# Gate and up blocks of an encoder layer: third and fourth products summed in a bank of their own

## The chip, the cores and the metric

The kernel runs on one core of a Trainium2 chip. The core has five engines that run their own instruction queues in order: PE (TensorE, matrix products), DVE (VectorE), ACT (ScalarE), POOL (GpSimd) and SP (SyncE, which here only issues DMAs). PE's weight loads have rows of their own, PEld. Products land in PSUM, in banks of 128 x 512 float32 values. The metric is the device time of one execution in microseconds (us).

## The reference, cut to what matters

One layer of a hybrid encoder works on two sequences of 512 tokens by 1024 channels. It starts and ends with a SwiGLU feed-forward step of 2816 hidden channels; between them lies a mixing stage (attention and a matrix memory) that the change does not touch.

```python
def swiglu(x, w_gate, w_up, w_down):
    return (jax.nn.silu(x @ w_gate) * (x @ w_up)) @ w_down
...
x = x + 0.5 * swiglu(rms_norm(x, ffn1_norm), ffn1_w_gate, ffn1_w_up, ffn1_w_down)
...
x = x + 0.5 * swiglu(rms_norm(x, ffn2_norm), ffn2_w_gate, ffn2_w_up, ffn2_w_down)
```

## The kernel before

Matrices are kept as a high and a low part in a reduced float32 type, and one product of values costs three matmuls (high by high, high by low, low by high). `product` (line 333) makes one block product: 4 slices of 128 channels by 3, so 12 matmuls of 128x512 into one bank.

Gate and up are computed together by a scheme of seven products in place of eight for a 2 x 2 block product: the two sequences are the two columns, the halves of the 1024 channels the inner index, and gate and up the two rows. The seven are called B11, B21, B22, T1, T2, T3 and T4. A block is 128 of the 2816 hidden channels; there are 22 blocks, and each feed-forward step runs them all before its down phase (line 589), which reads the products' sides back from HBM (`rbuf`).

For ten of the blocks, 0 to 9, B11 and B21 are computed early, while the inputs of the others are still being prepared, and parked in HBM (`kept`). Their turn later is called a *resumed* block here: its parked pieces v1 and g0 are loaded and it computes five products, T2, T1, T3, B22, T4. The other twelve, *computed* blocks, run all seven: B11, T2, B21, T1, T3, B22, T4. `ORDER` alternates the two kinds (0, 10, 1, 11 ... 7, 17), then come 18 to 21, computed, and 8 and 9, resumed.

`gu_rest` sums a block. It has three banks of PSUM pools: X (pool "mm", three buffers, `MM`) for B11 and B21, Y (pool "s", named pss, two buffers, `PS`) and Z (pool "t", named pst, two buffers, `PT`). One more pool, "o" (named pso, one buffer, `PO`), is used by the mixing stage and by the down phase. In a timeline X reads mm, Y pss and Z pst; T4's rows are those whose weights are called f.

The steps that the prediction names, all in `gu_rest`: line 364 (DVE) adds v1 and Y; line 368 (ACT) copies Z, with T1 in it, to v5; line 372 (DVE) adds the bank with T3 to v5; line 374 adds v1 to v5; line 377 (DVE) makes u2 from the bank Z, which by then holds T1 and B22; line 382 (DVE) adds the bank with T4 to v1; lines 383 and 384 multiply gate and up. Lines 291 and 292 split weights into high and low parts on ACT and DVE, lines 314 to 320 make their sums and differences, line 672 and 673 split T4's weights (and down weights), lines 396 and 397 split the block's results for the down phase and 398 and 399 store them through SP, and 403 to 415 form sums of the results of two blocks.

A scheduler orders each engine's queue from estimated times and priorities; the steps under `shifted(SOONER)` come ahead of others that are ready, those under `shifted(LATER)` behind. SP's queue carries the loads and stores.

Of the kernel before, what the change touches and what calls it, by code (L numbers as in the profile page):

```python
# [12 lines left out]
ALU = mybir.AluOpType  # L13
# [13 lines left out]
def encoder(ctx, tc, I, outs):  # L27
# [14 lines left out]
    def nm(s):  # L42
        n_id[0] += 1
        return f"{s}_{n_id[0]}"

    @contextmanager
    def shifted(n):

        tc.cur_priority += n
        yield  # L50
        tc.cur_priority -= n
# [58 lines left out]
    def PO():  # L110
        return po_.tile([P, S], F32, tag="o", name=nm("pso"))

    def PS():
        return ps.tile([P, S], F32, tag="s", name=nm("pss"))

    def PT():
        return pt.tile([P, S], F32, tag="t", name=nm("pst"))
# [149 lines left out]
    V_ = nc.vector  # L267
# [3 lines left out]
    B11, B21, B22, T4, T1, T2_, T3 = range(7)  # L271
# [29 lines left out]
    def w8_tile():  # L301
        return wpool.tile([P, 2, 2, HK_, P], F32R, tag="w8", bufs=4, name=nm("w"))

    def gu_left_a(rg, pin=lambda i: i):

        wa = w8_tile()
        w_pair(wa, rg.rearrange("p (a k) c -> p a k c", a=2), pin)
        return {B11: part(wa, 0), B21: part(wa, 1)}
# [20 lines left out]
    def product(p, w, xt, first):  # L329
        wh, wl = w  # L330
        for k in range(HK_):
            for i, (a, b) in enumerate(((wh, 0), (wh, 1), (wl, 0))):
                nc.tensor.matmul(p, a[:, k, :], xt[:, b, k, :], start=(first and k == 0 and i == 0),  # L333
                                 stop=(k == HK_ - 1 and i == 2), skip_group_check=True)

    def gu_first_a(W, xc, v1):

        X = MM()
        product(X, W[B11], xc[B11], True)
        with shifted(SOONER):  # L340
            nc.scalar.activation(v1, X, AF.Copy)
        return X

    def gu_first_b(X, W, xc, g0):

        product(X, W[B21], xc[B21], False)
        with shifted(SOONER):
            nc.scalar.activation(g0, X, AF.Silu)

    def gu_rest(W, xc, got, ring, mid):  # L350

        Y, Z = PS(), PT()
        second = lambda: product(Y, W[T2_], xc[T2_], True)
        if got:
            v1, g0 = got
            second()
        else:
            v1, g0 = ring("v"), ring("h")
            X = gu_first_a(W, xc, v1)
            second()  # L360
            gu_first_b(X, W, xc, g0)
        u2 = ring("h")
        with shifted(SOONER):
            V_.tensor_tensor(u2, v1, Y, op=ALU.add)  # L364
        product(Z, W[T1], xc[T1], True)
        v5 = ring("v")
        with shifted(SOONER):
            nc.scalar.activation(v5, Z, AF.Copy)  # L368
        mid()
        product(Y, W[T3], xc[T3], False)  # L370
        with shifted(SOONER):
            V_.tensor_tensor(v5, v5, Y, op=ALU.add)
        with shifted(SOONER):
            V_.tensor_tensor(v5, v5, v1, op=ALU.add)
        product(Z, W[B22], xc[B22], False)
        with shifted(SOONER):
            V_.tensor_tensor(u2, u2, Z, op=ALU.add)
        with shifted(SOONER):
            nc.scalar.activation(u2, u2, AF.Silu)
        product(Y, W[T4], xc[T4], False)  # L380
        with shifted(SOONER):
            V_.tensor_tensor(v1, v1, Y, op=ALU.add)
        V_.tensor_tensor(g0, g0, v1, op=ALU.mult)
        V_.tensor_tensor(u2, u2, v5, op=ALU.mult)
        return g0, u2
# [40 lines left out]
    class Up:  # L426
# [34 lines left out]
        def rest(self, raw, at=None, hook=None):  # L461
# [12 lines left out]
            for i, j in enumerate(ORDER):  # L474
                W = left
                nxt = ORDER[i + 1] if i + 1 < NF else None
                if nxt is not None:
                    left = {} if nxt in self.kept else gu_left_a(raw[0])
                    left.update(gu_left_b(*raw, ring))
                    ru = raw[1]  # L480
                    raw = self.fetch(ORDER[i + 2]) if i + 2 < NF else None
                then = []
                h = gu_rest(W, self.xc, got, ring, lambda: then.append(resume(nxt)) if nxt in self.kept else None)
                got = then[0] if then else None
                if nxt is not None:
                    left.update(gu_left_c(ru, ring))
                if i % 2 == 0:
                    sides = Sides(self.rb[i // 2], ring)
                    with shifted(LATER):
                        sides.even(*h)  # L490
                elif i < NF - 1:
                    sides.odd(*h)
                if i == at:
                    hook(h[0])
# [748 lines left out]
    xc = [None] * 7  # L1243
# [100 lines left out]
    W = [w8_tile() for _ in range(2)]  # L1344
# [15 lines left out]
    W = [{B11: part(w, 0), B21: part(w, 1)} for w in wt]  # L1360
# [11 lines left out]
    def second(j):  # L1372
        product(X[j], W[j][B21], xc[B21], False)
# [90 lines left out]
    xc = [None] * 7  # L1464
# [27 lines left out]
    W = [gu_left_a(raw0[0])]  # L1492
# [140 lines left out]
```

## Time and profile before

| | us |
|---|---|
| median of three runs | 2075.32 (2074.75 to 2075.62) |
| profiled execution | 2074.45 |
| its span | 2072.7 |
| PE busy | 2059.4 (99%) |
| DVE busy | 1544.9 (75%) |
| ACT busy | 903.3 (44%) |
| first gate and up stage, from the first T2 of a resumed block | 76.1 to 443 |
| second gate and up stage, likewise | 1481.6 to 1848 |

A row of a timeline has the start and the length in us, engine, line and operation, the tile written and the tiles read, shapes, and how many equal instructions it joins (x12); idle time of the engine ahead of a row stands in brackets, with what ended it. A matmul's length is drawn to its end, past the start of the next one, so lengths of neighbours overlap and starts tell the pace. In a view of waits a row names who waited (engine, tile, line), for whom, the total in us, how often, and the longest.

### The profile page before, as it was taken

How to read it: one execution, taken by the hardware profiler on the slowest of the kernel's cores; microseconds unless marked ns; L12 is line 12 of the kernel's file. 1: busy time of each engine (PE TensorE's matmuls, PEld its weight loads, DVE VectorE, ACT ScalarE, POOL GpSimd, SP SyncE). 2: the span in 40 equal slices, each digit the busy share in tenths (PEclk: the TensorE clock that was granted, in tenths of full speed). 3: DMA queues.
4: the chain of work that ended last, by engine and by line, in shares of the span. 5: the costliest groups of instructions: out<-in, count | busy, mean ns of one | idle time of the engine just before them, and what ended most of it. 6: DMA issues, size and time to landing. Idle time of an engine off the chain costs nothing.

```text
span 2072.7 us, 27121 instructions
## 1 busy us (share of the span) xinstructions
PE 2059.4 (99%) x9454; PEld 1689.0 (81%) x9454; DVE 1544.9 (75%) x2783; ACT 903.3 (44%) x1649; POOL 101.7 (5%) x117
## 2 busy tenths in 40 slices
PE   9999999999999999999999999999999999999998
PEld 7888888888888877888878788888888888888887
DVE  7888988786797897675567646555888888796697
ACT  7544444443234566463345443324544444443224
POOL 0000000001003000000120000002000000000001
PEclk9999999999999999999999999999999999999999
DMA  9555655699766655767684345677656555599753
GB/s 317 180 193 174 209 169 179 209 343 355 263 224 245 213 156 179 263 233 272 209 282 165 106 150 189 206 254 243 205 170 215 185 181 183 169 347 347 272 204 122
DMA packets 308104, 454.84 MB, mean 219 GB/s; under 512 B 20072, under 2 KB 179904, under 8 KB 306944
## 3 DMA queue, kind: packets, MB, share of 16 engines
q1 hardware_dynamic: 305968, 447.39, 64.0%
q0 software_dynamic: 1840, 5.46, 0.8%
q8 instruction: 74, 1.21, 0.2%
q14 instruction: 62, 0.51, 0.1%
q10 hardware_dynamic: 160, 0.27, 0.0%
HBM read 286.15 MB, written 166.89 MB: 219 GB/s over the span
## 4 chain that ended last, share of the span: by engine, by line
PE 97%; DVE 1%; DMA 1%; ACT 1%; issue 0%; ACTq 0%
PE mm L771 21%; PE pss L333 18%; PE pst L333 12%; PE mm L333 11%; PE mm L589 8%; PE pst L589 4%; PE pss L589 4%; PE mm L755 4%; PE pso L589 3%; PE pss L1018 1%; PE pso L1045 1%; PE pso L755 1%; PE pst L1037 1%; PE pso L1181 1%; PE pst L771 1%; PE pss L771 1%
## 5 line engine op out<-in xcount | busy, mean ns | idle before, releaser
L771 PE MATMUL mm<-xh,w 128*128 128x512 f32 x896 | 290.4, 394 | 0.0
L333 PE MATMUL mm<-xc,w 128*128 128x512 f32 x1056 | 254.5, 392 | 2.9 <-DVE w L292 1.6
L333 PE MATMUL pss<-xc,w 128*128 128x512 f32 x1056 | 256.0, 391 | 0.0
L333 PE MATMUL pst<-xc,w 128*128 128x512 f32 x1056 | 253.8, 389 | 0.0
L333 PEld LDWEIGHTS mm<-xc,w 128*128 128x128 f32 x1056 | 198.5, 189 | 45.6 <-DVE w L292 2.0
L333 PEld LDWEIGHTS pss<-xc,w 128*128 128x128 f32 x1056 | 197.0, 188 | 46.7 <-DVE t L364 6.1
L333 PEld LDWEIGHTS pst<-xc,w 128*128 128x128 f32 x1056 | 198.2, 188 | 41.5 <-ACT t L368 0.4
L771 PEld LDWEIGHTS mm<-xh,w 128*128 128x128 f32 x896 | 167.7, 188 | 33.5
L589 PE MATMUL mm<-rt,w 128*128 128x512 f32 x765 | 178.9, 389 | 0.0
L771 PE MATMUL mm<-xl,w 128*128 128x512 f32 x448 | 176.3, 394 | 0.0
L589 PEld LDWEIGHTS mm<-rt,w 128*128 128x128 f32 x765 | 143.5, 188 | 29.8
L291 ACT ACTIVATE w<-t 128x512 fp32r<-128x512 f32 x176 | 106.8, 627 | 136.4 <-issue 55.2
L292 DVE TENSOR_TENSOR w<-t,w 128x512 fp32r<-128x512 f32 x176 | 117.9, 687 | 55.3 <-ACT w L291 53.4
L333 PE MATMUL pss<-xc,f 128*128 128x512 f32 x528 | 126.8, 389 | 0.0
L333 PEld LDWEIGHTS pss<-xc,f 128*128 128x128 f32 x528 | 99.1, 188 | 20.6
L672 ACT ACTIVATE w<-wr 128x512 fp32r<-128x512 f32 x72 | 45.1, 632 | 138.5 <-PE pso L589 64.9
L672 ACT ACTIVATE w<-t 128x512 fp32r<-128x512 f32 x82 | 51.8, 632 | 107.3 <-PE pst L589 62.4
L771 PEld LDWEIGHTS mm<-xl,w 128*128 128x128 f32 x448 | 84.3, 188 | 16.7
L589 PE MATMUL pss<-rt,w 128*128 128x512 f32 x396 | 93.7, 389 | 0.0
L589 PE MATMUL pst<-rt,w 128*128 128x512 f32 x396 | 93.7, 389 | 0.0
L239 ACT ACTIVATE w<-wr 128x1024 fp32r<-128x1024 f32 (+1 forms) x56 | 57.3, 1028 | 73.5 <-PE mm L771 30.3
L589 PEld LDWEIGHTS pss<-rt,w 128*128 128x128 f32 x396 | 74.3, 188 | 15.4
(379 smaller groups left out, 3649.5 us busy)
## 6 DMA issues: line engine op xcount, KB each, us to landing
rt<-rbuf SPq DMA_DIRECT2D x154, 512.0 KB, 5.5
wpark<-w SPq DMA_DIRECT2D x104, 512.0 KB, 3.5
w<-wpark SPq DMA_DIRECT2D x104, 512.0 KB, 4.6
wr<-in_ffn_w_gate_dram SPq DMA_DIRECT2D x62, 512.0 KB, 5.3
rbuf<-tab SPq DMA_DIRECT2D x102, 256.0 KB, 3.8
wr<-in_ffn_w_up_dram SPq DMA_DIRECT2D x44, 512.0 KB, 4.4
rbuf<-f SPq DMA_DIRECT2D x72, 256.0 KB, 4.0
wr<-in_w_in_dram SPq DMA_DIRECT2D x36, 512.0 KB, 6.0
```

The lines of the kernel that those rows point to most:

```text
L239: pin(nc.scalar.activation(hi, raw, AF.Copy))
L291: pin(nc.scalar.activation(t[:, 0], src, AF.Copy))
L292: pin(V_.tensor_tensor(t[:, 1], src, f(t[:, 0]), op=ALU.subtract))
L333: nc.tensor.matmul(p, a[:, k, :], xt[:, b, k, :], start=(first and k == 0 and i == 0), stop=(k == HK_ - 1 and i == 2), skip_group_check=True)
L589: nc.tensor.matmul(p, u[:, a, d * P:(d + 1) * P], r[:, b, ts], start=(first and q == 0 and k == 0), stop=(q == len(us) - 1 and k == 2), sk ...
L672: nc.scalar.activation(hi, src, AF.Copy)
L755: nc.tensor.matmul(p[b][:, :N], a[:, k, bs], w_[:, kl, :], start=(k == 0 and i == 0), stop=(k == KD - 1 and i == 2))
L771: nc.tensor.matmul(p, a[:, k, :], b, start=(k == 0 and i == 0), stop=(k == n - 1 and i == 2))
L1018: nc.tensor.matmul(p, qT[:, h, b * P:(b + 1) * P], kv[:, hk * 2 + j, :], start=(j == 0), stop=(j == 1))
L1037: nc.tensor.transpose(p[:, b * P:(b + 1) * P], Ps[b][:, kb * P:(kb + 1) * P], ident)
L1045: nc.tensor.matmul(po, Vst[:, kv_, hk, :], w, start=(kv_ == 0 and i == 0), stop=(kv_ == 3 and i == 1))
L1181: nc.tensor.matmul(po, vm[:, a, t, hs_], b, start=(t == 0 and n == 0), stop=(t == 3 and n == 2))
```

## The change

`gu_rest` takes a third bank, T, from the pool "o". T3 begins a sum in T instead of going on in Y on top of T2, and T4 goes on in T. Since T2 is then not in the bank that T3 and T4 are summed in, it has to reach v5 and the last sum through v1: line 364 adds Y into v1 in place, where it wrote u2, and line 377 reads v1, where it read u2. The number of products, adds and copies is the same, and the lines keep their numbers.

```diff
-        Y, Z = PS(), PT()
+        Y, Z, T = PS(), PT(), PO()
...
         with shifted(SOONER):
-            V_.tensor_tensor(u2, v1, Y, op=ALU.add)
+            V_.tensor_tensor(v1, v1, Y, op=ALU.add)
         product(Z, W[T1], xc[T1], True)
...
-        product(Y, W[T3], xc[T3], False)
+        product(T, W[T3], xc[T3], True)
         with shifted(SOONER):
-            V_.tensor_tensor(v5, v5, Y, op=ALU.add)
+            V_.tensor_tensor(v5, v5, T, op=ALU.add)
         with shifted(SOONER):
             V_.tensor_tensor(v5, v5, v1, op=ALU.add)
         product(Z, W[B22], xc[B22], False)
         with shifted(SOONER):
-            V_.tensor_tensor(u2, u2, Z, op=ALU.add)
+            V_.tensor_tensor(u2, v1, Z, op=ALU.add)
...
-        product(Y, W[T4], xc[T4], False)
+        product(T, W[T4], xc[T4], False)
         with shifted(SOONER):
-            V_.tensor_tensor(v1, v1, Y, op=ALU.add)
+            V_.tensor_tensor(v1, v1, T, op=ALU.add)
```

On PE, the queue at the resumed block 1, the third block of the first stage, reads so before (T2, T1, one matmul of the next block's B11, T3, B22, the start of T4):

```order
L333 MATMUL pss_1212<-xc_318,w_1048 128x512 x12
L333 MATMUL pst_1213<-xc_557,w_1048 128x512 x12
L333 MATMUL mm_1314<-xc_316,w_1191 128x512
L333 MATMUL pss_1212<-xc_558,w_1049 128x512 x12
L333 MATMUL pst_1213<-xc_559,w_1049 128x512 x12
L333 MATMUL pss_1212<-xc_560,f_9_265 128x512 x2
```

And with the change:

```order
L333 MATMUL pss_1214<-xc_318,w_1049 128x512 x12
L333 MATMUL pst_1215<-xc_557,w_1049 128x512 x12
L333 MATMUL pso_1216<-xc_558,w_1050 128x512 x12
L333 MATMUL pst_1215<-xc_559,w_1050 128x512 x12
L333 MATMUL pso_1216<-xc_560,f_9_265 128x512 x2
```

T3 and T4 stand in pso, and the single matmul of B11 between T1 and T3 is gone; all 12 of B11 now follow T4. The same holds at seven resumed blocks of each stage; at block 8 of each stage it was one matmul of block 9's T2 that stood there.

On DVE, the queue at the same block, from the tail of the block before to L372, before:

```order
L397 TENSOR_TENSOR tab_279<-t_17_273,tab_279 128x512
L292 TENSOR_TENSOR w_1194<-t_6_262,w_1194 128x512
L411 TENSOR_TENSOR t_17_273<-t_17_273,t_14_270 128x512
L320 TENSOR_TENSOR t_6_262<-wr_1062,t_6_262 128x512
L364 TENSOR_TENSOR t_14_270<-t_12_268,pss_1212 128x512
L397 TENSOR_TENSOR f_19_275<-t_16_272,tab_279 128x512
L397 TENSOR_TENSOR t_15_271<-t_15_271,f_20_276 128x512
```

And with the change:

```order
L397 TENSOR_TENSOR tab_279<-t_17_273,tab_279 128x512
L364 TENSOR_TENSOR t_12_268<-t_12_268,pss_1214 128x512
L411 TENSOR_TENSOR t_17_273<-t_17_273,t_14_270 128x512
L292 TENSOR_TENSOR w_1196<-t_6_262,w_1196 128x512
L397 TENSOR_TENSOR f_19_275<-t_16_272,tab_279 128x512
L320 TENSOR_TENSOR t_6_262<-wr_1063,t_6_262 128x512
L397 TENSOR_TENSOR t_15_271<-t_15_271,f_20_276 128x512
```

L364 (t_12 is v1) moves up three places, and L292 and L320, weights of the next computed block, move down two each. What follows, from there to L372, stands as before; a little later L377 and L384 move up one place. ACT's queue is the same row for row; outside these blocks the queues of PE and DVE differ only at the closing blocks 8 and 9 of each stage, where L364 moves up in block 8 and down by one place in block 9. On SP's queue 14 pairs of neighbouring stores (lines 398 and 399) trade places.

## The prediction

> **What bounds the kernel now.** I read the page's first and fourth parts, then the waits of the weight-load engine, then PE's rows in time around one of those waits, then DVE's rows at the same place.
>
> ```profile
> span 2072.7 us, 27121 instructions
> PE 2059.4 (99%) x9454; PEld 1689.0 (81%) x9454; DVE 1544.9 (75%) x2783; ACT 903.3 (44%) x1649; POOL 101.7 (5%) x117
> PE 97%; DVE 1%; DMA 1%; ACT 1%; issue 0%; ACTq 0%
> ```
>
> PE is the bound: busy 99% of the span, and 97% of the chain that ended last. The rest of DVE, ACT and the queues counts only where PE waits for it. But "busy" hides short stalls, because a 128x512 matmul is drawn 0.39 us long while the next one starts 0.227 us later. So stalls are read from PEld's waits and from starts.
>
> ```profile
> PEld pss L333 <- DVE t L364: 6.1, 16, 0.4
> PEld pst L333 <- ACT t L368: 0.4, 1, 0.4
> ```
>
> Columns: total us, times, longest. Of the products of gate and up (line 333), 16 wait for L364, the add that reads Y before T3 may write into Y again. No other read of a product bank in these stages is waited for, but for one 0.4 us wait on L368. Here is PE in a computed block and the resumed block after it, up to the computed block that follows:
>
> ```profile
> 97.90 2.88 PE L333 MATMUL pst<-xc,w 128*128 128x512 f32 x12
> 100.62 2.88 PE L333 MATMUL pss<-xc,w 128*128 128x512 f32 x12
> 103.34 2.88 PE L333 MATMUL pst<-xc,w 128*128 128x512 f32 x12
> 106.06 2.88 PE L333 MATMUL pss<-xc,f 128*128 128x512 f32 x12
> 108.78 2.88 PE L333 MATMUL pss<-xc,w 128*128 128x512 f32 x12
> 111.50 2.88 PE L333 MATMUL pst<-xc,w 128*128 128x512 f32 x12
> 114.22 0.39 PE L333 MATMUL mm<-xc,w 128*128 128x512 f32 x1
> 114.58 3.06 PE L333 MATMUL pss<-xc,w 128*128 128x512 f32 x12
> 117.47 2.88 PE L333 MATMUL pst<-xc,w 128*128 128x512 f32 x12
> 120.19 2.88 PE L333 MATMUL pss<-xc,f 128*128 128x512 f32 x12
> 122.91 2.65 PE L333 MATMUL mm<-xc,w 128*128 128x512 f32 x11
> 114.58 1.48 PEld L333 LDWEIGHTS pss<-xc,w 128*128 128x128 f32 x7 [0.39 <-DVE t L364]
> ```
>
> From start to start every product of 12 takes 2.72 us (0.2267 a matmul), in all rows but two. The single matmul at 114.22, borrowed from the next block, and T3 at 114.58 take 117.47 - 114.22 = 3.25 us for 13 matmuls, where 13 x 0.2267 = 2.95: 0.30 lost. In the computed block T3 (100.62) follows T1 (97.90) without loss.
>
> Why L364 is late: DVE has had no idle time since L382, 4 us before (a row with idle time ahead of it carries it in brackets).
>
> ```profile
> 109.64 0.68 DVE L382 TENSOR_TENSOR t<-t,pss 128x512 f32<-128x512 f32 x1
> 112.64 0.68 DVE L411 TENSOR_TENSOR t<-t,t 128x512 f32<-128x512 f32 x1
> 113.25 0.68 DVE L320 TENSOR_TENSOR t<-wr,t 128x512 f32<-128x512 f32 x1
> 113.85 0.68 DVE L364 TENSOR_TENSOR t<-t,pss 128x512 f32<-128x512 f32 x1
> 116.85 0.68 DVE L415 TENSOR_TENSOR t<-t,t 128x512 f32<-128x512 f32 x1
> 117.67 0.69 DVE L372 TENSOR_TENSOR t<-t,pss 128x512 f32<-128x512 f32 x1
> ```
>
> T2 ended at about 111.5 and L364 started at 113.85, in its turn of the queue; T3's first weights load at 114.58, just as it ends (114.53).
>
> **The change, part by part.** *T3 leaves Y: the wait goes.* Its price is best read from the distance of like rows. Between the single-matmul rows of two resumed blocks lie 144 matmuls, 32.64 us at 0.2267. First and last of seven such rows in each feed-forward part, and the two resumed blocks that close the parts:
>
> ```profile
> 311.75 0.39 PE L333 MATMUL mm<-xc,w 128*128 128x512 f32 x1
> 1519.71 0.39 PE L333 MATMUL mm<-xc,w 128*128 128x512 f32 x1
> 1717.22 0.39 PE L333 MATMUL mm<-xc,w 128*128 128x512 f32 x1
> 420.86 3.26 PE L333 MATMUL pss<-xc,w 128*128 128x512 f32 x13
> 423.96 0.84 PE L333 MATMUL pst<-xc,w 128*128 128x512 f32 x3
> 1826.30 3.29 PE L333 MATMUL pss<-xc,w 128*128 128x512 f32 x13
> 1829.43 0.39 PE L333 MATMUL pst<-xc,w 128*128 128x512 f32 x1
> ```
>
> First part: 311.75 - 114.22 = 197.53 over six distances, less 6 x 32.64 = 195.84, is 1.69, or 0.282 a place; second: 197.51 - 195.84 = 1.67, 0.278. Seven places each: 1.97 + 1.95. The closing ones: 423.96 - 420.86 = 3.10 and 3.13, less 2.95: 0.15 + 0.18. Sum 4.25 us at 16 places, the 16 of the wait view. That view's 6.1 us is the upper end. It counts idle weight load, and the matmul at 114.22 runs on for 0.39 us beside the first of it; so I take 4.25, nearest to the rows of starts.
>
> The Trainium skill ("TensorE: Matmul & The Clock Gate", "Architectural detail") says that TensorE's queue can pull a weight load ahead of matmuls in flight. By it a weight load's wait is only partly PE time, 4.25 and not 6.1; the trace agrees, with 3.25 us for 13 matmuls beside a weight-load wait of 0.39.
>
> *What T3 waits for now.* T has one buffer, so T3 waits for L382 of the block before. That row ends at 110.32 and T3 could start at 114.22: 3.9 us in hand today. After a resumed block B11 and B21 add two products, so more. Price 0.
>
> *T4 follows T3 in T.* It waits for L372, as before. L372 ends at 118.36, T4 starts at 120.19: 1.83 in hand. With the stall gone T3 starts at 114.22 and T4 at 114.22 + 24 x 0.2267 = 119.66, while DVE, busy until 117.53, cannot run L372 earlier than about 117.6. In hand 1.3: price 0, and this is what is late next. At its end lies the whole gain given back.
>
> *T3 begins a sum in place of continuing one.* T1 begins a sum (97.90), T3 continues one (100.62); both 2.72. Price 0.
>
> *L364 writes v1 in place, L377 takes v1 and writes u2.* Two operands and one result as before: L364 separate takes 0.68, L372 in place 0.69. At most 0.01 on a DVE that has 4.8 us free in a pair of blocks:
>
> ```profile
> 279.20:312.10 32.90, 32.90 (x145) 26.93 (x144) 28.08 (x45) 14.33 (x25) 0.00 (x0) 1.00 0.59 191
> ```
>
> (32.90 us, of which DVE is busy 28.08.) With 0.28 less per pair, 4.5 stay free: DVE does not become the bound.
>
> *Order.* L364 moves up three places on DVE, so L292 (weights of the next computed block) and L320 come two instructions, 1.2 us, later. The next block's T2, the first to use them, starts after T3, B22, T4 and B11, 11 us on: price 0. The borrowed matmul of B11 goes back behind T4; the same number runs: 0. The stores of side pieces trade places on SP's queue, for data that is read only after the last block: 0.
>
> *The end of the first part*, where the other wait stands:
>
> ```profile
> 434.61 2.88 PE L333 MATMUL pss<-xc,w 128*128 128x512 f32 x12
> 437.49 3.02 PE L333 MATMUL pst<-xc,w 128*128 128x512 f32 x12
> 436.31 0.63 ACT L672 ACTIVATE w<-wr 128x512 fp32r<-128x512 f32 x1 [4.11 <-DMA wr<-in_ffn_w_down_dram]
> 436.85 0.58 ACT L368 ACTIVATE t<-pst 128x512 f32<-128x512 f32 x1
> 430.92 0.80 SPq L531 DMA_DIRECT2D wr<-in_ffn_w_down_dram  x2
> 430.20 0.68 DVE L673 TENSOR_TENSOR f<-wr,f 128x512 fp32r<-128x512 f32 x1
> 429.42 0.64 ACT L672 ACTIVATE f<-wr 128x512 fp32r<-128x512 f32 x1 [1.19 <-PE pss L333]
> ```
>
> L368 stands behind a split that waits for a load of the down weights. Read upwards from the last row, that load goes back to PE: T4 of block 8 ends, ACT and DVE split the next weights, the raw buffer is free, the load starts. A PE that comes 2.1 us sooner starts it sooner, so this stall stays. If the load's time were fixed by other traffic instead, the first part's 2.1 us would be lost; I take 0 and keep that end.
>
> **Sum.** 4.25 off. The profiled execution took 2074.45 us with a span of 2072.7, 0.87 under the median of 2075.32; so 2070.2 for such an execution and 2071.1 for the median.
>
> **The rivals.**
> - *Half comes back*: the load at 430.92 holds its time, or T4 waits for L372 at half of the places. For it: 1.3 us in hand is little, and DVE is packed there. Against: L372 keeps its place behind the same work. About 2.1 lost: 2073.2.
> - *More than the sum*: all 6.1 of the wait view is PE time. Against: the starts. 2069.2.
> - *The change does nothing*: T3 at the same places waits for something that was hidden behind L364 (its weights, say). Against: T3 of the computed block starts at once. 2075.3.
> - *Slower*: the single buffer T. If L382 ran so late that it ended 4.26 us after its present place, T3 (114.58 - 110.32) would wait; from 4.54 on, 7.6 instructions of 0.6, the wait costs more than the 0.28 saved. Eight instructions late is 0.54 at 16 places, 8.7 - 4.25 = 4.4 us more: 2079.7. Against: it would need L382 to drop behind all the splits of the next block, and it stays ahead of L673 in the new order.
>
> **How the numbers follow.** Stall gone 0.80, half back 0.07, more 0.04, nothing 0.03, slower 0.06. A change under 0.2% (4.15 us) is about what a measurement can't tell from none. The forecast, 4.25, lies on that bound, and the three runs spread by 0.87 (2074.75 to 2075.62), so I count 0.62 of the first case beyond it: faster 0.80 x 0.62 + 0.04 = 0.54; same 0.30 + 0.07 + 0.03 = 0.40; slower 0.06. The likeliest case alone is 2070.3 to 2071.9. The range, 2070.0 to 2073.3, takes in half back.
>
> **What would show it.** In the changed profile PEld's wait for L364 is gone; resumed blocks' like rows lie 32.64 us apart in place of 32.92; T3 follows T1 by 2.72 everywhere; PEld waits for neither L372 nor L382; the wait for L368 near 435 stays at 0.4. A wait of T4 for L372, a longer one for L368, or T3 waiting for L382 makes the prediction wrong.

## The result and the profile after

The changed kernel takes 2070.2 us (median of 13 runs, 2069.6 to 2073.7), the kernel before 2074.86 (13 runs): 4.66 us less, a ratio of 0.9979 with a 95% interval of 0.9972 to 0.9986. The profiled execution of the changed kernel has a span of 2068.1, against 2072.7.

The head of its page:

```profile
span 2068.1 us, 27136 instructions
PE 2055.5 (99%) x9454; PEld 1690.9 (82%) x9454; DVE 1542.6 (75%) x2783; ACT 901.4 (44%) x1649; POOL 99.7 (5%) x117
```

PE is busy 99% of the span as before, so this line would not have shown what was lost or won. The Trainium skill ("Perfetto Trace Analysis", "Identifying the Most-Contended Engine") warns that matmul busy time measures closeness to the limit badly, since matmuls are pipelined. The trace agrees: 2059.4 of 2072.7 and 2055.5 of 2068.1 are the same share, though the second kernel is 4.6 us shorter.

What changed stands in the waits of the weight loads of line 333. With the change these are all of them:

```profile
PEld mm L333 <- DVE xc L1332: 1.4, 2, 0.7
PEld mm L333 <- DVE w L292: 1.3, 1, 1.3
PEld mm L333 <- ACT xc L1346: 1.2, 1, 1.2
PEld mm L333 <- ACT f L341: 0.6, 2, 0.4
PEld pst L333 <- ACT t L368: 0.2, 1, 0.2
```

The 16 waits for L364 (6.1 us) are gone. None for L372 or L382 has come. PE and DVE at resumed block 1, the place shown before:

```profile
108.33 2.88 PE L333 MATMUL pss<-xc,w 128*128 128x512 f32 x12
111.05 2.88 PE L333 MATMUL pst<-xc,w 128*128 128x512 f32 x12
113.77 2.88 PE L333 MATMUL pso<-xc,w 128*128 128x512 f32 x12
116.49 2.88 PE L333 MATMUL pst<-xc,w 128*128 128x512 f32 x12
119.21 2.88 PE L333 MATMUL pso<-xc,f 128*128 128x512 f32 x12
109.19 0.68 DVE L382 TENSOR_TENSOR t<-t,pso 128x512 f32<-128x512 f32 x1
111.59 0.68 DVE L364 TENSOR_TENSOR t<-t,pss 128x512 f32<-128x512 f32 x1
117.00 0.68 DVE L372 TENSOR_TENSOR t<-t,pso 128x512 f32<-128x512 f32 x1
```

Every product starts 2.72 us after the one before it, T3 too. L364 ends at 112.27, 1.5 us before T3 starts. L372 ends at 117.68, 1.53 before T4.

To see the stages whole: from the start of the first T2 to the start of the last T4 of a stage there are 133 products, 1596 matmuls, 361.76 us at 0.22667. The first and last rows of both stages before, and after (there with the row ahead of the last one of the first stage, which is needed further down):

```profile
76.14 2.88 PE L333 MATMUL pss<-xc,w 128*128 128x512 f32 x12
440.35 2.88 PE L333 MATMUL pss<-xc,f 128*128 128x512 f32 x12
1481.63 2.88 PE L333 MATMUL pss<-xc,w 128*128 128x512 f32 x12
1845.52 2.88 PE L333 MATMUL pss<-xc,f 128*128 128x512 f32 x12
```

```profile
75.69 2.88 PE L333 MATMUL pss<-xc,w 128*128 128x512 f32 x12
434.73 2.99 PE L333 MATMUL pst<-xc,w 128*128 128x512 f32 x12
437.55 2.88 PE L333 MATMUL pso<-xc,f 128*128 128x512 f32 x12
1479.22 2.88 PE L333 MATMUL pss<-xc,w 128*128 128x512 f32 x12
1840.98 2.88 PE L333 MATMUL pso<-xc,f 128*128 128x512 f32 x12
```

Before, the first stage took 440.35 - 76.14 = 364.21, so 2.45 was lost in it; the second took 363.89 and lost 2.13. After, 361.86 and 361.76: 0.10 and 0.00. That is 4.48 of the 4.6 us by which the spans differ. Read in the same way, the kernels of the experiments give:

| kernel | first T2 at | lost in stage 1 | lost in stage 2 | from stage 1 to stage 2 | after stage 2 |
|---|---|---|---|---|---|
| before | 76.14 | 2.45 | 2.13 | 1041.28 | 227.15 |
| before, again | 75.26 | 2.21 | 2.12 | 1041.09 | 227.16 |
| computed blocks only | 76.05 | 2.26 | 2.24 | 1042.07 | 227.23 |
| after | 75.69 | 0.10 | 0.00 | 1041.67 | 227.13 |
| after, again | 75.84 | 0.00 | 0.00 | 1042.05 | 227.13 |
| late add | 75.70 | 0.00 | 0.00 | 1042.07 | 227.19 |
| same bank | 75.41 | 0.00 | 0.00 | 1041.17 | 227.20 |
| resumed blocks only | 75.71 | 0.00 | 0.00 | 1041.91 | 227.12 |
| late last add | 76.75 | 1.67 | 2.29 | 1043.49 | 228.08 |

The two columns on the right hold the time from the last T4 of stage 1 to the first T2 of stage 2, and from the last T4 of stage 2 to the end.

### The profile page after: what moved, and what is told of

Same layout as the page of the kernel before. It is cut to its first block, busy times and chain, and to the rows that moved or that the text cites. A ratio compares the mean times of both kernels' runs of the same rounds, so it can differ in the third digit from the quotient of the medians.

```text
span 2068.1 us, 27136 instructions
## 1 busy us (share of the span) xinstructions
PE 2055.5 (99%) x9454; PEld 1690.9 (82%) x9454; DVE 1542.6 (75%) x2783; ACT 901.4 (44%) x1649; POOL 99.7 (5%) x117
## 4 chain that ended last, share of the span: by engine, by line
PE 97%; DVE 1%; DMA 1%; ACT 1%; issue 0%; SPq 0%; DVEq 0%; ACTq 0%
PE mm L771 21%; PE pst L333 12%; PE pso L333 12%; PE mm L333 11%; PE mm L589 8%; PE pss L333 6%; PE pss L589 4%; PE pst L589 4%; PE mm L755 4%; PE pso L589 3%; PE pss L1018 2%; PE pso L1045 1%; PE pso L755 1%; PE pst L1037 1%; PE pso L1181 1%; PE pst L771 1%
## 5 line engine op out<-in xcount | busy, mean ns | idle before, releaser
L292 DVE TENSOR_TENSOR w<-t,w 128x512 fp32r<-128x512 f32 x176 | 118.2, 689 | 53.2 <-ACT w L291 51.4
L333 PE MATMUL pso<-xc,w 128*128 128x512 f32 x528 | 126.8, 389 | 0.0
L333 PE MATMUL pss<-xc,w 128*128 128x512 f32 x528 | 126.8, 389 | 0.0
L333 PE MATMUL pso<-xc,f 128*128 128x512 f32 x528 | 126.8, 389 | 0.0
L333 PEld LDWEIGHTS pso<-xc,f 128*128 128x128 f32 x528 | 99.2, 188 | 20.5
L333 PEld LDWEIGHTS pso<-xc,w 128*128 128x128 f32 x528 | 99.2, 188 | 20.5
L333 PEld LDWEIGHTS pss<-xc,w 128*128 128x128 f32 x528 | 99.1, 188 | 20.5
```

The source lines that it names most:

```text
L292: pin(V_.tensor_tensor(t[:, 1], src, f(t[:, 0]), op=ALU.subtract))
```

## The experiments

Two theories were set against each other. In the *bank theory*, the one of the prediction, T3 waits because it shares Y with T2, and leaving Y is what helps. In the *order theory* the add L364 came too late only because of where it stood on DVE; by writing into v1 in place it moves up, and the third bank adds nothing.

**The changed kernel again.** No edit.

> The changed kernel once more, beside the next three. Bank theory (T3's wait for L364 cost 4.25 us, and leaving Y removes it) and order theory (L364, writing in place, moves up three places, and Y is read in time) both: 4.2 to 4.7 us under the kernel before, about 2070.3 against 2074.9. Gate and up stages at 0.2267 us a matmul, with less than 0.3 us lost in each. The changed profile had 0.45 us less before the first stage and 0.39 us more in the mixing stage than the one before; if these belong to the execution and not to the change they come out otherwise here.

2070.26 against 2075.01, ratio 0.9978 (0.9969 to 0.9987). Nothing is lost in either stage. The time ahead of the first stage (75.84) and between the stages (1042.05) lies within what unchanged parts show from one execution to another (75.3 to 76.1, 1041.1 to 1042.1 in the table without the last row). So these two are no effect of the change.

**Late add.** The third bank stays, L364 goes back to its old place.

```diff
-        with shifted(SOONER):
+        with shifted(0):
             V_.tensor_tensor(v1, v1, Y, op=ALU.add)
```

> The changed kernel with L364's priority lowered, so that L364 stands again behind L292, L411 and L320 as in the kernel before; T3 and T4 stay in T. Bank theory: T3 doesn't wait though L364 is late; no wait of weight loads for L364, time as the changed kernel, 2070.3. Order theory: the gain needs L364's new place; the 16 waits are back, 2074.6 to 2074.9.

2070.25, ratio 0.9977 (0.9967 to 0.9987): the whole gain. PE and DVE at the same block:

```profile
111.06 2.88 PE L333 MATMUL pst<-xc,w 128*128 128x512 f32 x12
113.78 2.88 PE L333 MATMUL pso<-xc,w 128*128 128x512 f32 x12
116.50 2.88 PE L333 MATMUL pst<-xc,w 128*128 128x512 f32 x12
112.20 0.69 DVE L411 TENSOR_TENSOR t<-t,t 128x512 f32<-128x512 f32 x1
112.81 0.69 DVE L320 TENSOR_TENSOR t<-wr,t 128x512 f32<-128x512 f32 x1
113.41 0.68 DVE L364 TENSOR_TENSOR t<-t,pss 128x512 f32<-128x512 f32 x1
```

L364 ends at 114.09, when T3 is 0.3 us under way in T. That is 3.03 us after T1's start, just as in the kernel before (114.53 and 111.50). So the bank is enough by itself, and an add as late as before costs nothing then. This holds at seven resumed blocks of each stage, 14 of the 16 places. At block 8 of each stage L364 ends 1.1 us after T1's start in this run, where it ended 2.9 after it before; the bank alone is not tried there.

One more difference goes along with the stalls: at these 14 places a single matmul of the next block's B11 stands between T1 and T3 in every kernel that has them, and in none that hasn't. It is not what T3 waited for. In the kernel before, T3's first weight load starts 0.05 us after L364 ends (114.58 and 114.53), and 0.36 after that matmul's start.

**Same bank.** The add in place stays, the third bank goes. T3 begins a new sum in Y.

```diff
-        Y, Z, T = PS(), PT(), PO()
+        Y, Z = PS(), PT(); T = Y
```

> The changed kernel with T = Y: L364 adds into v1 in place, T3 begins a new sum in Y, no third bank; every engine's order is that of the changed kernel. Bank theory taken strictly: T3 still has to wait for L364, and part of the loss stays, up to 2074.9. Order theory: L364 ends some 1.5 us before T1 does (111.59 + 0.68 against 113.77 in the changed profile), so nothing waits: 2070.3. If both this and the run with the late add come out at 2070.3, either part of the change is enough by itself.

2070.38, ratio 0.9976 (0.9966 to 0.9985): the whole gain again.

```profile
110.77 2.88 PE L333 MATMUL pst<-xc,w 128*128 128x512 f32 x12
113.49 2.88 PE L333 MATMUL pss<-xc,w 128*128 128x512 f32 x12
116.21 2.88 PE L333 MATMUL pst<-xc,w 128*128 128x512 f32 x12
111.31 0.68 DVE L364 TENSOR_TENSOR t<-t,pss 128x512 f32<-128x512 f32 x1
111.91 0.68 DVE L411 TENSOR_TENSOR t<-t,t 128x512 f32<-128x512 f32 x1
```

T3 follows T1 by 2.72 us in the very bank that L364 reads, since L364 has ended at 111.99. So the add in place is enough by itself too. It is ahead of L411 now. In the queue before, L364 wrote u2's row t_14, and L411, two places ahead of it, reads t_14: a result of older blocks was still in use there. Writing into v1 needs no such row. The trace shows that dependence. In the view of line 364, DVEq stands for DVE's queue itself; a row has the number of waits and the shortest, median and longest in ns. The kernel before, then the late add:

```profile
L364 DVEq EVENT_SEMAPHORE  x38: 21/36/1097, 79.8 to 1836.0; - x38
L364 DVEq EVENT_SEMAPHORE  x20: 21/21/21, 79.1 to 1833.2; - x20
```

Before, at each of the 16 places the queue waits on behalf of L364, 0.60 us at 14 of them and 1.10 at the two of block 8, and each wait ends 0.05 us after L411. With the late add L364 stands behind L411 too, but writes v1, and never waits more than 0.02. That the scheduler placed L364 late for this reason follows from the dependence and from the edits; no run freed the row alone.

**Computed blocks only, resumed blocks only.** The change made in one kind of block, by `got`, which is set in resumed blocks; here for resumed ones, and with the two sides of each choice swapped for computed ones.

```diff
-        Y, Z, T = PS(), PT(), PO()
+        Y, Z = PS(), PT(); T = PO() if got else Y
...
-            V_.tensor_tensor(v1, v1, Y, op=ALU.add)
+            V_.tensor_tensor(v1 if got else u2, v1, Y, op=ALU.add)
...
-        product(T, W[T3], xc[T3], True)
+        product(T, W[T3], xc[T3], bool(got))
...
-            V_.tensor_tensor(u2, v1, Z, op=ALU.add)
+            V_.tensor_tensor(u2, v1 if got else u2, Z, op=ALU.add)
```

> The third bank and the add in place in computed blocks alone; resumed blocks as before. Every engine's order is that of the kernel before. Both theories: computed blocks had no wait to lose, the 16 waits for L364 stay at 6 us in all, time as before, 2074.9. Rival (a sum begun in a bank of its own is cheaper by itself, wait or not): 12 of 22 blocks gain, about 2072.4.

> The third bank and the add in place in resumed blocks alone; computed blocks as before. Both theories: the whole gain, 2070.3. Rival (part of the gain comes from the computed blocks): 2072.4.

Computed only: 2074.87 against 2075.01, ratio 1.0 (0.9991 to 1.0009). Its waits:

```profile
PEld pss L333 <- DVE t L364: 6.3, 17, 0.4
```

The 17th is a wait of 0.17 us at block 0 of the first stage that cost 0.03.

Resumed only: 2070.11 against 2074.23, ratio 0.9981 (0.9972 to 0.9989), and no row of line 333 waits for L364. The whole gain comes from the resumed blocks, and a bank of its own has no worth where T3 did not wait.

**Late last add.** The changed kernel with L382, the last read of T, moved back on DVE.

```diff
-        with shifted(SOONER):
+        with shifted(2 * LATER):
             V_.tensor_tensor(v1, v1, T, op=ALU.add)
```

> The changed kernel with L382 (the read of T after T4) at a lower priority: in resumed blocks the L382 of the block before now stands in the place on DVE's queue where L364 stood in the kernel before, 4.2 us later than in the changed one. Theory of the single buffer (the rival on the slower side, at its deciding point): T3 waits for L382 at most of the 16 places, about 0.3 us each, the gain is given back, 2074 to 2075.5, with weight loads of pso waiting for L382. If T were free regardless, 2070.3.

2077.34 against 2074.23, ratio 1.0014 (1.0005 to 1.0023): slower than the kernel before, and more than was expected.

```profile
PEld pso L333 <- DVE t L382: 5.2, 14, 0.7
```

```profile
112.11 2.88 PE L333 MATMUL pst<-xc,w 128*128 128x512 f32 x12
114.83 0.39 PE L333 MATMUL mm<-xc,w 128*128 128x512 f32 x1
112.65 0.68 DVE L364 TENSOR_TENSOR t<-t,pss 128x512 f32<-128x512 f32 x1
113.25 0.68 DVE L320 TENSOR_TENSOR t<-wr,t 128x512 f32<-128x512 f32 x1
113.85 0.68 DVE L397 TENSOR_TENSOR t<-t,f 128x512 fp32r<-128x512 f32 x1
114.45 0.68 DVE L382 TENSOR_TENSOR t<-t,pso 128x512 f32<-128x512 f32 x1
115.18 0.99 PEld L333 LDWEIGHTS pso<-xc,w 128*128 128x128 f32 x5 [0.39 <-DVE t L382]
```

With L382 of the block before ending at 115.13, T3 has the stall that it had for L364, at 14 places. The stages lose 1.67 and 2.29, about the old loss; in the second figure are one longer wait for L382 (0.67) and one of 0.4 for L368. More is lost behind the stages: the down phase now waits at its start, in both halves of the kernel, for weights that ACT and DVE split too late:

```profile
453.90 2.26 PE L589 MATMUL mm<-rt,w 128*128 128x512 f32 x8 [0.65 <-ACT w L672]
1861.29 2.02 PE L589 MATMUL mm<-rt,w 128*128 128x512 f32 x7 [0.49 <-ACT w L672]
```

By the starts of the down phase's matmuls this costs 1.10 and 0.93 us, where the eight other traces lose nothing there; in the table the middle and last parts are 1.4 and 0.9 us over the longest of the others. The first T2 also comes 0.6 us later than in any other trace, which no run explains. So the single buffer T is a real limit; it is off the path only because L382 is early.

**The kernel before, again.** No edit.

> The kernel before, once more. 2074.9; the 16 waits at 6.1 us again, 2.1 to 2.45 us lost in each gate and up stage. What differs from the first profile outside these stages is what one execution differs from another.

2074.49 against 2074.23, ratio 1.0 (0.9991 to 1.0009):

```profile
PEld pss L333 <- DVE t L364: 6.1, 16, 0.4
```

The same 16 waits. But the wait for L368 near 435 us, worth 0.3 us in the first profile, is not in this one; its stages lose 2.21 and 2.12.

## Why the prediction was right, and where it was not

- *The wait and its price.* Right: 16 waits, all in resumed blocks, and the gain lies near the 4.25 us by starts, not the 6.1 of the weight loads' waits. Summed over every matmul's start, the 16 stalls come to 4.28 us in the first profile of the kernel before and to 4.29 in its second. The stages lost 4.33 to 4.58 us in the three traces that have the waits, and 0.00 to 0.10 in the five that have neither these waits nor the late last add. The 4.48 of the first pair of profiles is more than 4.28 because of the end of the first stage (last point of this list). The timed difference was 4.66 in the first comparison, 4.75, 4.76 and 4.63 for three kernels without the waits on one chip and 4.12 for one on another; what is over or under 4.3 is within what the front and middle parts vary by.
- *The time.* For the median 2071.1 was summed, and 2070.2 came, 0.1 under the likeliest case's lower end. About half of the 0.9 is the starting point: the kernel before has a median of 2074.86 over 13 runs, not the 2075.32 of three. The other half is the gain, 4.66 and not 4.25. The line of 0.2% (4.15 us), on which the chances of "faster" and "same" were split, lies inside the interval of the measured ratio (0.14% to 0.28%), so the result does not decide between these two; a change of nothing lies outside.
- *T3's new wait for L382.* Right: L382 (109.19 and 0.68 long) ends 3.9 us ahead of T3's start at 113.77 in the changed kernel, and no wait came. The rival on the slower side was sized at L382's place: brought to the deciding point it gave the stalls back as told. What neither it nor the expectation of that run counted is the start of the two down phases, where with L382 later the splits came too late: another 2.0 us.
- *T4 behind T3.* 1.3 us in hand was forecast, 1.53 measured, and PE never waited there.
- *A new sum and the add in place cost nothing.* Right: 2.72 a product, 0.68 an add.
- *Order costs nothing.* Right for the time. But two things were read wrongly. L364 was called late by its turn in a packed queue; it also waited for L411, which still read u2's row, and could not stand ahead of it. And its new place was booked as a side effect at price 0, though it removes the wait by itself, as the run with the same bank shows. The change holds two remedies for one stall, and the prediction credited one.
- *The end of the first stage.* It was forecast that the wait for L368 stays at 0.4, at price 0. It was 0.2 in the changed profile, and none in its second one or in the second of the kernel before, so it belongs to the execution and not to either kernel. By starts it cost 0.30 before (440.35 - 434.61 = 5.74, less 24 x 0.2267 = 5.44) and 0.10 after (437.55 - 434.73 = 2.82, less 2.72): 0.2 of the first pair's 4.48 came by luck. From the load's issue to the split that waits for it and stands ahead of L368 it took 5.39 and 5.42 us in the two profiles with the wait, and 5.03 and 4.36 in the second ones without. The rival that the load holds its time is refuted: it was issued at 430.92 before and at 428.09 after.

## What to carry to other kernels

Where matmul rows overlap, busy time hides stalls of a few tenths of a microsecond; take the distance of equal rows and the pace of an undisturbed stretch. When a product waits for the read of its bank, ask both what else could hold the product and what keeps the read late: here the add was to write a row that was still being read, which an add in place avoids without another bank. A single-buffered bank is free only as long as its last read stays early, so the read's place in the queue is part of the design.

## What was not expected of the hardware

After a stall the matmuls do not fall back to their pace at once. In the profile before, from the start of T3 at 114.58 to the start of the next product it took 2.89 us where 2.72 is usual, though its only wait was ahead of the first matmul; the changed kernel and the two that undo one half of it show 2.72 for the same product. A weight load that waited 0.39 us so cost 0.30 us of PE time: 0.13 ahead of T3's first matmul, 0.11 between the first and the second, and 0.06 over the next ten distances, which are 0.224 to 0.240 us. The 0.11 is in part no slower pace: T3's first weights (0.19 us to load) begin to load at 114.58, just where their matmul is drawn to start, while for the single matmul ahead the load began at 114.00 and the matmul at 114.22. What slows the later ones no run shows.
